# Second score pass of an attention kernel: 64 contraction rows, two chunks on two row tiles

## The chip, the cores and the metric

The kernel runs on one core of a Trainium2 chip. The metric is the device time of one execution in microseconds (us). The engines are named as in the profile: PE is TensorE's matmul side, PEld its weight loads, DVE is VectorE, ACT is ScalarE, POOL is GpSimd, SP is SyncE, which issues nearly all DMAs here.

## The reference, cut to what matters

The program is a two-layer trunk over 1024 latent and 256 context tokens of width 1024. Layer 0 is a recurrent unit beside a spatial gating unit; layer 1 is a gated convolution beside differential attention. Only the attention's scores are touched. There are 4 heads; each has two score maps (m = 0 and 1) with a head dimension of 64, and all 1280 tokens as keys:

```python
def diff_attention(q, k, v, lam):
    s = jnp.einsum('bqhmd,bkhmd->bhmqk', q, k).astype(jnp.float32) * (DIFF_HEAD_DIM ** -0.5)
    p = jax.nn.softmax(s, axis=-1)
    a = p[:, :, 0] - lam * p[:, :, 1]
    return jnp.einsum('bhqk,bkhe->bqhe', a.astype(v.dtype), v)
```

## The kernel before, in words

Every float32 operand of a large matmul is split into two halves that the array takes at its fast float32r rate: a high half (the value rounded, by an ACT copy) and a low half (the value less the high half, by DVE or POOL). A product is then three passes, high by high, high by low and low by high.

The scores use the small head dimension for this. `load_k` (L885 to L892) loads the 64 rows of a head's map twice, into partitions 0 to 63 and again into 64 to 127 of `kd`. An ACT copy rounds all 128 rows into `kt` (L890), and DVE then overwrites rows 64 to 127 with the low half (L891). So `kt` holds the high half of the keys over their low half. `load_q` (L902 to L910) doubles the query rows in the same way, and splits them into `qh` and `ql`, which have the same 64 rows twice. One matmul of `qh` against `kt` over 128 rows therefore sums query-high by key-high and query-high by key-low.

`scores(i, m, st)` (L935 to L952) makes the scores of 128 queries against 1280 keys in one PSUM tile `psc`, of which there is one buffer. The keys go in three chunks, of 256, 512 and 512 columns (`CHUNKS`, L28). For each chunk a matmul with `qh` (L942) is followed by one with `ql` (L943), both over all 128 rows. Then DVE takes the row maximum of all 1280 columns (L944), and ACT the exponentials into `e` (L946). The next call writes `psc` again, so its first matmul waits until ACT has read it.

The loop at L1013 runs over 32 blocks of 128 queries, i, with two calls of `scores` each, and two more rounds for the pipeline's end. That is 64 calls. Between the calls stand the transposes of the combined maps (`trans`, L954), the product with the values (`av`, L968), and `fill(us)` (L916). `fill` takes steps of three matmuls from the other projections of layer 1 (generators of `proj1_g`, L174 to L176) until a fixed budget of time, written in `FL`, is used up. The budgets are constants. What the fillers have left at the end runs behind the attention (L1068). `load_k` of the next head is called behind a head's last two calls of `scores`.

TensorE's instructions run in the order in which they are written (`manual_schedule`, L55). The other engines' order is chosen by the framework's own timeline at build.

Elsewhere in the program, in layer 0, some small matmuls take part of the array's columns: `mod_mm` (L208 to L211) puts four matmuls with 32 weight columns each on four column tiles (`tile_position=(0, r)`), and L462 (`gatep`) has 2 weight columns. They stand between the large matmuls of layer 0's projections, as the steps of a generator do.

Of the kernel before, what the change touches and what calls it, by code (L numbers as in the profile page):

```python
# [11 lines left out]
F32R = mybir.dt.float32r  # L12
AF = mybir.ActivationFunctionType
# [14 lines left out]
CHUNKS = ((0, 256), (256, 512), (768, 512))  # L28
# [14 lines left out]
def tile_hybrid_trunk(es: ExitStack, tc: tile.TileContext, A, out, scr=None):  # L43
    nc = tc.nc
    V, S, G, T, SY = nc.vector, nc.scalar, nc.gpsimd, nc.tensor, nc.sync

    def pool(name, space=None, **kw):
        if space is not None:
            kw["space"] = space
        return tc.tile_pool(name=name, bufs=1, reuse_waits="tile", **kw)  # L50

    def f32(ap):
        return ap.bitcast(F32)
# [189 lines left out]
        split(hi, lo, raw, le=le)  # L243
        return hi, lo

# [1 line left out]
    pj_cm = pool("pj", PSUM)  # L247
    pj = pj_cm.__enter__()

    def pj3(name):  # L250
        t = pj.tile([128, 1536], F32, name=name, tag="pj", bufs=2)
        return t
# [77 lines left out]

    WC = 1282

# [1 line left out]
    lru_cm = ExitStack()  # L334
    lb, ld = lru_cm.enter_context(pool("lrub")), lru_cm.enter_context(pool("lrud"))
    with pool("lrua") as lp, pool("lruc") as lc:
# [167 lines left out]
        p = pj3("pu")  # L504
# [3 lines left out]
        while blocks or late:  # L508
            mod_step()

# [1 line left out]
    vp_cm = pool("sguv", side="right")  # L512
    vp = vp_cm.__enter__()
    so_cm = tc.manual_schedule(engines={nc.sync.engine})
# [5 lines left out]
    p = pj3("pz")  # L520
# [9 lines left out]
    with pool("sguw") as vw:  # L530
# [52 lines left out]
        p = pj3("pu")  # L583
# [72 lines left out]
        G.tensor_tensor(bs[:, 15:16], bs[:, 14:15], cm05[:, 0:1], op=ALU.pow)  # L656
        return bs[:, 12:13], bs[:, 15:16]

# [1 line left out]
    g1 = const.tile([128, KT, 2], F32, name="g1")  # L660
    b1 = const.tile([128, KT, 2], F32, name="b1")
    V.tensor_tensor(g1, mod1[:, :, 1, :], P("lng0")[:, :, None].to_broadcast([128, KT, 2]), op=ALU.mult)
# [66 lines left out]
    woa_cm.__exit__(None, None, None)  # L729
    po_cm.__exit__(None, None, None)  # L730

# [1 line left out]
    mask = [(i + 16) % 32 for i in range(32)]  # L733
    pa_cm, pb_cm = pool("pa", PSUM), pool("pb", PSUM)
    pbp, pa = pb_cm.__enter__(), pa_cm.__enter__()
# [1 line left out]
    def pb(name):  # L737
        t = pbp.tile([128, 512], F32, name=name, tag="pb", bufs=2)
        return t
# [64 lines left out]
    for t in range(NT):  # L804
        p = pb("pv")
# [5 lines left out]
    kv_cm.__exit__(None, None, None)  # L811
    hc_cm.__exit__(None, None, None)

# [1 line left out]
    def proj_qg(hd):  # L815
        w = wload(A["w_in1"][16 + hd])
        qf = rt("qf")
        for c0 in (0, 512):
            p = pb("pq")
            yield from proj1_g(p, w, CTX + c0, 512)  # L820
            x = qf[:, c0:c0 + 512]
            S.activation(x, p, AF.Copy, scale=0.125)
            rope(x, c0, pp)
            SY.dma_start(q_d[hd][:, c0:c0 + 512], x)
        w = wload(A["w_in1"][24 + hd])
        sg = cs.tile([128, LAT], F32, name="sg8", tag="sg8", bufs=1)
        for c0 in (0, 512):
            p = pb("pg8")
            yield from proj1_g(p, w, CTX + c0, 512)
            s = sg[:, c0:c0 + 512]  # L830
            S.activation(s, p, AF.Tanh, scale=0.5)
            V.scalar_tensor_tensor(s, s, 1.0, p, op0=ALU.add, op1=ALU.mult)
            SY.dma_start(g_d[hd][:, c0:c0 + 512], s)
# [37 lines left out]
    ap = ab_cm.__enter__()  # L871
# [13 lines left out]
    def load_k(hd, m):  # L885
        kd = ap.tile([128, NTOK], F32, name="kd", tag="kd", bufs=1)
        for i in range(2):
            SY.dma_start(kd[64 * i:64 * i + 64], k_d[hd][64 * m:64 * m + 64])
        kt = ap.tile([128, NTOK], F32R, name=f"k{m}")
        S.activation(kt, kd, AF.Copy)  # L890
        V.tensor_tensor(kt[64:128], kd[64:128], f32(kt[64:128]), op=ALU.subtract)  # L891
        KS[m] = kt  # L892

    def load_v(hd):
        vf = ap.tile([128, NT, 128], F32, name="vf", tag="kd", bufs=1)
# [28 lines left out]
    KS, VS, QS, AH, OF, SD = {}, {}, {}, {}, {}, {}  # L924
# [10 lines left out]
    def scores(i, m, st):  # L935
        hd, pr, u = i // 8, i % 8 // 2, i % 2
        qh, ql = QS[hd, pr]
        cu = slice(128 * u, 128 * u + 128)
        p = pa.tile([128, 1536], F32, name="psc", tag="psc", bufs=1)
        for c, n in CHUNKS:  # L940
            o = p[:, 256 + c:256 + c + n]
            T.matmul(o, qh[:, m, cu], KS[m][:, c:c + n], start=True, stop=False)  # L942
            T.matmul(o, ql[:, m, cu], KS[m][:, c:c + n], start=False, stop=True)  # L943
        V.tensor_reduce(st[:, m:m + 1], p[:, 256:1536], axis=AX.X, op=ALU.max, negate=True)  # L944
        e_ = ap.tile([128, NTOK], F32, name="e", tag="e", bufs=3)
        S.activation(e_, p[:, 256:1536], AF.Exp, bias=st[:, m:m + 1], scale=1.0, accum_out=st[:, 2 + m:3 + m])  # L946
        if m == 1:
            V.reciprocal(st[:, 5:6], st[:, 3:4])
            V.scalar_tensor_tensor(st[:, 6:7], st[:, 5:6], st[:, 2:3], nlam, op0=ALU.mult, op1=ALU.mult)
            V.scalar_tensor_tensor(SD[i // 4][:, i % 4:i % 4 + 1], st[:, 2:3], EPS, st[:, 2:3], op0=ALU.mult,  # L950
                                   op1=ALU.mult)
        return e_  # L952
# [54 lines left out]
    run(proj_qg(0))  # L1007
    fillers += [proj_qg(1), conv_branch(0), proj_qg(2), conv_branch(1), proj_qg(3), conv_branch(2), conv_branch(3)]
    load_k(0, 0)
    load_k(0, 1)  # L1010
    load_v(0)
    E0, fin = {}, None
    for i in range(34):  # L1013
        hd, pr, u = i // 8, i % 8 // 2, i % 2
        if i < 32:
            if u == 0:
                QS[hd, pr] = load_q(hd, pr)
            st = ap.tile([128, 8], F32, name="st", tag="st", bufs=3)
            if i % 4 == 0:
                SD[i // 4] = ap.tile([128, 4], F32, name="sd", tag="sd", bufs=2)  # L1020
            E0[i] = scores(i, 0, st)
            if i % 8 == 7 and hd < 3:
                load_k(hd + 1, 0)
# [17 lines left out]
        if i < 32:  # L1041
            e1 = scores(i, 1, st)
            V.scalar_tensor_tensor(E0[i], e1, st[:, 6:7], E0[i], op0=ALU.mult, op1=ALU.add)
            if i % 8 == 7 and hd < 3:
                load_k(hd + 1, 1)
# [25 lines left out]
    pa_cm.__exit__(None, None, None)  # L1071
    pb_cm.__exit__(None, None, None)

# [1 line left out]
    with pool("out1") as op, pool("po1", PSUM) as po:  # L1075
        rows = []
        for i, nm in enumerate(("ln_g", "ln_b")):
# [146 lines left out]
```

## Time and profile before

| what | value |
|---|---|
| median of 3 runs | 1170.76 us (1170.17 to 1171.86) |
| span of the profiled execution | 1170.5 us |
| PE busy, of the whole span | 1132.6 us (97%) |
| stretch of the attention | 630 to 1025 us, 395 us |
| PE busy there | 385.5 us |
| DVE, ACT and POOL busy there | 292.9, 196.6 and 84.8 us |

The stretch of the attention goes from shortly before the first call of `scores` to shortly behind the last transposes. A PE row's duration is longer than its distance to the next row, since matmuls are pipelined: what a matmul costs in a stream is the distance from start to start. A weight load stands in a row of PEld. In the page's groups a time of idling before an instruction, with the engine that ended it, stands behind the second bar.

### The profile page before, as it was taken

What the parts mean: (1) busy time and instruction counts of PE and PEld (TensorE: products, weight loads), DVE (VectorE), ACT (ScalarE), POOL (GpSimd) and SP (SyncE); (2) the same over time, 40 slices, a digit from 0 to 9 for tenths busy, and PEclk for the clock granted to TensorE, in tenths of its full rate; (3) what the DMA queues carried; (4) which work ended last, traced back from release to release, by engine and by line L of the source; (5) the groups of instructions that cost most, each with busy time, mean ns of one, the idle gap of its engine ahead of it and who ended that gap; (6) DMA issues with size and microseconds to landing.
All of it is one profiled execution on the core that took longest, in us unless ns stands there. A gap on an engine that the chain in (4) does not pass through costs nothing.

```text
span 1170.5 us, 14967 instructions
## 1 busy us (share of the span) xinstructions
PE 1132.6 (97%) x5842; PEld 922.0 (79%) x5842; DVE 738.9 (63%) x1007; ACT 440.2 (38%) x685; POOL 329.6 (28%) x200
## 2 busy tenths in 40 slices
PE   6999999899999999999999899999999999999997
PEld 3667777678888888888887788788888788888776
DVE  5677986943411475636104668876777877738897
ACT  3453654621121234342113455544544554413110
POOL 1114212620240132258104311221121321221971
PEclk9999999999999999999999999999999999999999
DMA  9654551230332444243215411322221510126622
GB/s 373 239 182 142 180 176 41 73 130 1 120 104 71 144 139 147 96 136 140 77 45 162 113 55 54 95 76 84 77 76 37 146 62 19 46 72 249 218 99 82
DMA packets 71606, 133.93 MB, mean 114 GB/s; under 512 B 6368, under 2 KB 34912, under 8 KB 70640
## 3 DMA queue, kind: packets, MB, share of 16 engines
q1 hardware_dynamic: 71536, 132.97, 34.3%
q8 instruction: 46, 0.75, 0.3%
q14 instruction: 24, 0.20, 0.1%
HBM read 105.67 MB, written 27.28 MB: 114 GB/s over the span
## 4 chain that ended last, share of the span: by engine, by line
PE 83%; DVE 8%; DMA 3%; ACT 3%; issue 2%; POOL 0%; SPq 0%; POOLq 0%; DVEq 0%; ACTq 0%
PE px L164 5%; PE pu L164 5%; PE pg L164 5%; PE p L174 5%; PE p L175 5%; PE p L176 5%; PE pout L648 4%; PE pout L646 4%; PE pout L647 4%; PE pz L164 4%; PE psc L942 3%; PE pv L198 3%; PE pv L199 3%; PE pv L200 3%; PE psc L943 3%; PE atr L965 3%
## 5 line engine op out<-in xcount | busy, mean ns | idle before, releaser
L141 POOL TENSOR_TENSOR wlo<-wraw,whi 128x512 fp32r<-128x512 f32 x92 | 148.1, 1615 | 458.5 <-ACT whi L138 449.8
L648 PE MATMUL pout<-woh,ylo 128*128 128x512 f32 (+1 forms) x296 | 114.5, 387 | 3.1 <-DVE ylo L141 3.1
L946 ACT ACTIVATE e<-psc,st 128x1280 f32<-128x1280 f32 x64 | 85.1, 1329 | 85.6 <-DVE st L944 85.6
L646 PE MATMUL pout<-woh,yhi 128*128 128x512 f32 (+1 forms) x296 | 114.8, 388 | 0.2
L647 PE MATMUL pout<-wol,yhi 128*128 128x512 f32 (+1 forms) x296 | 114.0, 385 | 0.0
L944 DVE TENSOR_REDUCE st<-psc 128x1 f32<-128x1280 f32 x64 | 95.0, 1485 | 27.8 <-PE psc L943 27.7
L138 ACT ACTIVATE whi<-wraw 128x512 fp32r<-128x512 f32 x92 | 57.2, 628 | 134.3 <-PE p L175 27.7
L174 PE MATMUL p<-hhl,whi 128*128 128x512 f32 x256 | 106.8, 417 | 0.0
L176 PE MATMUL p<-hhl,wlo 128*128 128x512 f32 x256 | 100.7, 393 | 0.0
L175 PE MATMUL p<-hll,whi 128*128 128x512 f32 x256 | 100.5, 393 | 0.0
L942 PE MATMUL psc<-k,qh 128*128 128x512 f32 (+1 forms) x192 | 68.0, 369 | 8.4 <-ACT e L946 8.4
L943 PE MATMUL psc<-k,ql 128*128 128x512 f32 (+1 forms) x192 | 69.3, 361 | 0.0
L138 ACT ACTIVATE ah<-atr 128x512 fp32r<-128x512 f32 (+1 forms) x96 | 48.5, 525 | 51.6 <-PE atr L965 50.6
L648 PEld LDWEIGHTS pout<-woh,ylo 128*128 128x128 f32 x296 | 55.6, 188 | 15.3 <-DVE ylo L141 4.0
L646 PEld LDWEIGHTS pout<-woh,yhi 128*128 128x128 f32 x296 | 55.6, 188 | 12.1 <-DVE zt L610 0.5
L647 PEld LDWEIGHTS pout<-wol,yhi 128*128 128x128 f32 x296 | 55.7, 188 | 11.5
L138 ACT ACTIVATE yhi<-yraw 128x512 fp32r<-128x512 f32 x36 | 22.5, 630 | 103.7 <-PE pout L647 57.6
L141 DVE TENSOR_TENSOR al<-atr,ah 128x512 fp32r<-128x512 f32 (+1 forms) x96 | 55.6, 594 | 5.8 <-ACT ah L138 5.6
L176 PEld LDWEIGHTS p<-hhl,wlo 128*128 128x128 f32 x256 | 48.2, 188 | 10.7
L175 PEld LDWEIGHTS p<-hll,whi 128*128 128x128 f32 x256 | 48.6, 190 | 7.3
L141 DVE TENSOR_TENSOR ylo<-yraw,yhi 128x512 fp32r<-128x512 f32 x36 | 43.2, 1208 | 17.5 <-ACT yhi L138 17.5
L174 PEld LDWEIGHTS p<-hhl,whi 128*128 128x128 f32 x256 | 48.4, 189 | 7.2
(292 smaller groups left out, 2822.2 us busy)
## 6 DMA issues: line engine op xcount, KB each, us to landing
wraw<-in_w_in_dram SPq DMA_DIRECT2D x44, 512.0 KB, 3.7
wm<-in_w_mod_dram SPq DMA_DIRECT2D x64, 256.0 KB, 3.4
wraw<-in_w_out_dram SPq DMA_DIRECT2D x16, 512.0 KB, 3.5
wm<-in_w_mod_dram SPq DMA_DIRECT2D x7, 1024.0 KB
xt<-in_xcT_dram SPq DMA_DIRECT2D x8, 640.0 KB, 9.8
xres<-in_xc_dram SPq DMA_DIRECT2D x10, 512.0 KB, 3.7
kd<-k_d SPq DMA_DIRECT2D x16, 320.0 KB, 4.7
wvr<-in_w_v_dram SPq DMA_DIRECT2D x8, 512.0 KB, 4.4
```

Of the source, the lines that this page charges most:

```text
L138: S.activation(hi, src, AF.Copy)
L141: le.tensor_tensor(lo, src, f32(hi), op=ALU.subtract)
L164: T.matmul(o, wt[:, k % 4], hh[hx][:, k], start=st, stop=sp_)
L174: T.matmul(o, hi[:, k % 4], hh[:, k], start=k == 0, stop=False)
L175: T.matmul(o, hi[:, k % 4], hl_[:, k], start=False, stop=False)
L176: T.matmul(o, lo[:, k % 4], hh[:, k], start=False, stop=k == KT - 1)
L646: T.matmul(o, hi[:, i], wh[:, c], start=first and i == 0, stop=False)
L647: T.matmul(o, hi[:, i], wl[:, c], start=False, stop=False)
L648: T.matmul(o, lo[:, i], wh[:, c], start=False, stop=not first and i == 3)
L942: T.matmul(o, qh[:, m, cu], KS[m][:, c:c + n], start=True, stop=False)
L943: T.matmul(o, ql[:, m, cu], KS[m][:, c:c + n], start=False, stop=True)
L944: V.tensor_reduce(st[:, m:m + 1], p[:, 256:1536], axis=AX.X, op=ALU.max, negate=True)
```

## The change

The second pass with `ql` of the two 512-column chunks is made over 64 rows, with the key's high half only. The product of the query's low half with the key's low half is left out there. The two matmuls are put on two row tiles of the array, the first on rows 0 to 63, the second on rows 64 to 127. As the second needs the key's high half in partitions 64 to 127, `load_k` makes one more tile `kx` by one more ACT copy of 512 columns. The 256-column chunk keeps its two matmuls over 128 rows. The six matmuls of a call are put in another order: the three with `qh`, the small one with `ql`, and then the two on row tiles.

```diff
         kt = ap.tile([128, NTOK], F32R, name=f"k{m}")
         S.activation(kt, kd, AF.Copy)
+        kx = ap.tile([128, 512], F32R, name=f"kx{m}")
+        S.activation(kx[64:128], kd[64:128, 768:1280], AF.Copy)
         V.tensor_tensor(kt[64:128], kd[64:128], f32(kt[64:128]), op=ALU.subtract)
-        KS[m] = kt
+        KS[m] = kt, kx
...
         p = pa.tile([128, 1536], F32, name="psc", tag="psc", bufs=1)
-        for c, n in CHUNKS:
-            o = p[:, 256 + c:256 + c + n]
-            T.matmul(o, qh[:, m, cu], KS[m][:, c:c + n], start=True, stop=False)
-            T.matmul(o, ql[:, m, cu], KS[m][:, c:c + n], start=False, stop=True)
+        kt, kx = KS[m]
+        o0, o1, o2 = (p[:, 256 + c:256 + c + n] for c, n in CHUNKS)
+        T.matmul(o1, qh[:, m, cu], kt[:, 256:768], start=True, stop=False)
+        T.matmul(o2, qh[:, m, cu], kt[:, 768:1280], start=True, stop=False)
+        T.matmul(o0, qh[:, m, cu], kt[:, 0:256], start=True, stop=False)
+        T.matmul(o0, ql[:, m, cu], kt[:, 0:256], start=False, stop=True)
+        T.matmul(o1, ql[0:64, m, cu], kt[0:64, 256:768], start=False, stop=True, tile_position=(0, 0))
+        T.matmul(o2, ql[64:128, m, cu], kx[64:128], start=False, stop=True, tile_position=(64, 0))
```

On PE, at one call of `scores` in the middle of the attention (`psc` the scores, `k` the key tile, rows L174 to L176 a filler's step), the order before is:

```order
L176 MATMUL p_6422<-hhl,wlo 128x512
L942 MATMUL psc<-k_5612,qh 128x256
L943 MATMUL psc<-k_5612,ql 128x256
L942 MATMUL psc<-k_5612,qh 128x512
L943 MATMUL psc<-k_5612,ql 128x512
L942 MATMUL psc<-k_5612,qh 128x512
L943 MATMUL psc<-k_5612,ql 128x512
L174 MATMUL p_6422<-hhl,whi 128x512
```

and with the change, at the same place:

```order
L176 MATMUL p_6430<-hhl,wlo 128x512
L944 MATMUL psc<-k_5616,qh 128x512
L945 MATMUL psc<-k_5616,qh 128x512
L946 MATMUL psc<-k_5616,qh 128x256
L947 MATMUL psc<-k_5616,ql 128x256
L948 MATMUL psc<-k_5616,ql 128x512
L949 MATMUL psc<-kx_5618,ql 128x512
L174 MATMUL p_6430<-hhl,whi 128x512
```

The number of matmuls is the same, six; the last two are those on row tiles, and what stands ahead of and behind the call is as it was.

On ACT, around a load of a head's keys (`k` the rounded keys, `kd` the loaded ones, `ah` a transposed map, `e` the exponentials), the order before is:

```order
L138 ACTIVATE whi<-wraw 128x512
L890 ACTIVATE k_5673<-kd 128x1280
L138 ACTIVATE ah<-atr 128x2x128
L138 ACTIVATE whi<-wraw 128x512
L946 ACTIVATE e,st<-psc,st 128x1280
```

and with the change:

```order
L138 ACTIVATE whi<-wraw 128x512
L890 ACTIVATE k_5679<-kd 128x1280
L892 ACTIVATE kx_5681<-kd 64x512
L138 ACTIVATE ah<-atr 128x2x128
L138 ACTIVATE whi<-wraw 128x512
L952 ACTIVATE e,st<-psc,st 128x1280
```

One copy is added directly behind that of `k`, eight times in all. The orders of SP and POOL are the same in both kernels, and DVE's differs in one transposed map's low half, which is one place later.

## Rows read from the trace of the kernel before

**Rows 1.** The page: engines' busy time, the chain's shares by engine, two groups.

```profile
PE 1132.6 (97%) x5842; PEld 922.0 (79%) x5842; DVE 738.9 (63%) x1007; ACT 440.2 (38%) x685; POOL 329.6 (28%) x200
...
PE 83%; DVE 8%; DMA 3%; ACT 3%; issue 2%; POOL 0%; SPq 0%; POOLq 0%; DVEq 0%; ACTq 0%
...
L946 ACT ACTIVATE e<-psc,st 128x1280 f32<-128x1280 f32 x64 | 85.1, 1329 | 85.6 <-DVE st L944 85.6
...
L944 DVE TENSOR_REDUCE st<-psc 128x1 f32<-128x1280 f32 x64 | 95.0, 1485 | 27.8 <-PE psc L943 27.7
```

**Rows 2.** Busy time by stretch, the attention: stretch and length, engines, clock, DMA.

```profile
630.00:1025.00 395.00, 385.50 (x2132) 326.75 (x2131) 292.90 (x409) 196.64 (x327) 84.76 (x55) 0.99 0.26 77
```

**Rows 3.** Who waited for whom, PE in the attention: total us, times, longest.

```profile
PE psc L942 <- ACT e L946: 8.4, 6, 4.8
PE prs L1002 <- POOL rr L994: 1.1, 1, 1.1
```

**Rows 4.** PE in order of time, one call: start, duration, instruction, idle before.

```profile
774.74 0.28 PE L942 MATMUL psc<-k,qh 128*128 128x256 f32 x1
774.86 0.28 PE L943 MATMUL psc<-k,ql 128*128 128x256 f32 x1
774.98 0.40 PE L942 MATMUL psc<-k,qh 128*128 128x512 f32 x1
775.21 0.40 PE L943 MATMUL psc<-k,ql 128*128 128x512 f32 x1
775.45 0.39 PE L942 MATMUL psc<-k,qh 128*128 128x512 f32 x1
775.67 0.40 PE L943 MATMUL psc<-k,ql 128*128 128x512 f32 x1
775.90 0.39 PE L174 MATMUL pq<-hhl,whi 128*128 128x512 f32 x1
```

**Rows 5.** PEld in order of time, the weight loads of the same call.

```profile
775.45 0.19 PEld L943 LDWEIGHTS psc<-k,ql 128*128 128x128 f32 x1
775.68 0.19 PEld L174 LDWEIGHTS pq<-hhl,whi 128*128 128x128 f32 x1
```

**Rows 6.** PE in order of time, a matmul pair with 2 weight columns, layer 0.

```profile
72.33 0.63 PE L164 MATMUL px<-hhl,wlo 128*128 128x512 f32 x2
72.89 1.02 PE L462 MATMUL gatep<-mb,par 128*2 128x512 f32 x2
73.84 0.38 PE L389 MATMUL pgate<-xh,whi 128*128 128x258 f32 x1
74.07 0.29 PE L390 MATMUL pgate<-xo,whi 128*128 128x258 f32 x1
```

**Rows 7.** PEld in order of time, the weight loads of the same place.

```profile
72.89 0.09 PEld L462 LDWEIGHTS gatep<-mb,par 128*2 128x2 f32 x2 [0.37 <-issue]
73.84 0.19 PEld L389 LDWEIGHTS pgate<-xh,whi 128*128 128x128 f32 x1 [0.86 <-ACT whi L138]
73.95 0.19 PEld L390 LDWEIGHTS pgate<-xo,whi 128*128 128x128 f32 x1
```

**Rows 8.** PE in order of time, matmuls on four column tiles between layer 0's.

```profile
102.76 0.63 PE L164 MATMUL px<-hhl,wlo 128*128 128x512 f32 x2
103.32 1.06 PE L211 MATMUL modp<-wm,csil 128*32 128x512 f32 x8
104.32 0.38 PE L164 MATMUL px<-hhc,whi 128*128 128x256 f32 x1
```

**Rows 9.** Groups on PE by shape: count, busy us, mean ns, idle before.

```profile
L942 PE MATMUL psc<-k,qh 128*128 128x256 f32 x64 | 19.8, 310 | 8.4 <-ACT e L946 8.4
L943 PE MATMUL psc<-k,ql 128*128 128x256 f32 x64 | 18.1, 283 | 0.0
```

**Rows 10.** Groups on ACT in the attention, columns as in rows 9.

```profile
L138 ACT ACTIVATE qh<-qd 128x512 fp32r<-128x512 f32 x16 | 10.1, 630 | 10.3 <-PE psc L942 7.7 <-issue 1.4 <-DMA qd<-q_d 1.2
```

**Rows 11.** Busy time by stretch, four short ones, columns as in rows 2.

```profile
642.00:646.60 4.60, 0.00 (x0) 0.00 (x0) 3.85 (x3) 1.31 (x2) 2.97 (x2) 0.99 0.23 63
646.60:650.00 3.40, 3.24 (x9) 2.66 (x10) 1.60 (x6) 0.60 (x3) 1.28 (x1) 0.51 0.85 215
756.50:758.40 1.90, 0.00 (x0) 0.00 (x0) 1.61 (x4) 1.46 (x3) 0.15 (x1) 1.00 0.90 243
...
759.20:766.00 6.80, 6.80 (x21) 5.66 (x20) 5.05 (x8) 2.53 (x4) 2.28 (x2) 0.50 0.23 66
```

## The prediction, made before the changed kernel ran

> **What bounds the kernel now.** I read the page first. PE is busy for 97% of the span and holds 83% of the chain that ended last [rows 1]. So a nanosecond of PE counts, as long as PE has other work to turn to. Next I read the stretch in which the scores lie. In 395 us of attention PE is busy for 385.5; DVE has 292.9, ACT 196.6 [rows 2]. The missing 9.5 us are nearly all explained by two waits: 8.4 us in six waits of a call's first matmul for ACT's exponentials of the call before, the longest 4.8, and 1.1 us once for POOL [rows 3]. The projections fill the time between the calls by a fixed budget, and what is left of them runs behind the attention. So what a call of `scores` takes or gives back on PE goes into the end time nearly one for one.
>
> The third view is one call, in order of time [rows 4]. From its first matmul to the next instruction behind it are 775.90 - 774.74 = 1.16 us. From start to start a 512-column matmul costs 0.23 us (0.92 for four) and a 256-column one 0.12. The durations of 0.40 and 0.28 are longer, since the end of one overlaps the next: a matmul starts some 0.17 us before the record of the one ahead ends (775.67 + 0.40 = 776.07, against 775.90). The weights are loaded ahead: those for the matmul at 775.90 begin at 775.68, while the matmul before runs [rows 5]. No weight load is on the path.
>
> **What the change saves.** Two second passes of 512 columns, 0.46 us, become two that may run side by side on two halves of the array. The nearest row for this is on column tiles: in layer 0 eight matmuls on four column tiles take 1.06 us [rows 8], where two of the same columns on a single tile take 1.02 [rows 6]. Six more matmuls cost 0.04, so some 0.01 for each further one beside the first. By that the pair costs 0.23 + 0.01 = 0.24 us and saves **0.22 us** a call, 14.1 us in 64 calls. The other four matmuls only change places, at no cost: all write PSUM ranges that the same call owns, and the first waits for ACT as before.
>
> **What the change adds on PE.** The array goes from whole to halves and back in each call. The trace of before has no row tile. It has the change to a part of the columns and back, in layer 0, and there it isn't free. The record of the last whole-array matmul ends at 72.33 + 0.63 = 72.96. The load for the 2-column matmul starts at 72.89, 0.07 us before that end [rows 6, 7]. In a stream the next matmul itself would have started 0.17 before. So 0.10 us are lost, and only then do the weights begin to load: PEld idles for 0.37 us with nothing to wait for but "issue" [rows 7]. On the way back it is the same. The pair's record ends at 72.89 + 1.02 = 73.91, the next load starts at 73.84, again 0.07 before. The matmul of 258 columns with these weights then lasts 0.38 us where the next one lasts 0.29 [rows 6]: it stands 0.10 us for its weights, as nothing was loaded ahead. The place with four column tiles reads alike: 102.76 + 0.63 = 103.39 against 103.32, and 0.38 us for the first matmul behind [rows 8]. One change of the array's form thus costs 0.10 + 0.10 = 0.20 us, with 128 columns of weights behind it. A call would have two, **0.40 us**.
>
> The bounds for a row tile's change are 0 (a stream goes on as in rows 5) and 0.20 us. I take 0.20: it is the only change of form that this trace shows, and it reads the same on the way in and out. The Trainium skill, in TensorEngine Tiling (Array Packing), section Tiling Modes (Key Properties), says that changing the tiling mode, not merely the tile, drains TensorE. That would extend the same cost to row tiles; no row here shows it for them. The sum by that page is the one by the upper bound.
>
> **The sum on PE.** A call goes from 1.16 to 1.16 - 0.22 + 0.40 = 1.34 us. In 64 calls +0.18 each are **+11.5 us**.
>
> **What is given back.** The 0.20 us on the way back lie between a call's last matmul and the next call, beside the DVE maximum (1.485 us) and ACT's exponentials (1.329 us, rows 1) on which that next call waits. The six waits shrink by up to 0.20 each, 1.2 us [rows 3]. Besides, a call's first matmul takes 310 ns in the mean where the second takes 283 [rows 9]: 27 ns by 64 are 1.7 us, where a late release kept the weights from being loaded ahead. With more slack I take half of that, 0.8. Together **-2.0 us**, with bounds of 0 and -2.9.
>
> **The extra copy.** `kx` is one ACT copy of 512 columns, eight times. The nearest row, a copy of that width, takes 630 ns [rows 10], so 5.0 us if all of it were on the path, and nothing if all is hidden. Queued behind it on ACT are a transposed map, a weight split or the exponentials of a call. ACT is busy for half of the attention [rows 2], and the next head's keys are loaded ahead of need, so I take **+0.5 us**. The buffer `kd` is held by DVE's longer subtraction anyway, and the DMA issues on SP keep their order. DVE's one instruction in another place has no price.
>
> In all 1170.5 + 11.5 - 2.0 + 0.5 = 1180.5 us for the profiled execution. The median of the runs is 0.3 us over its span, so I forecast **1180.8 us**, 0.9% slower.
>
> **Rivals.** *The change of form is free for row tiles (faster).* Both tiles take the whole width of the array in columns, and the weights could go into it ahead as in rows 5. The call then falls to 0.94 us, the waits stay, and the time is 1170.8 - 14.1 + 0.5 = 1157.2 us. The point at which the sign turns is 0.11 us for one change. For it speaks that every change seen here cuts the columns, not the rows. Against it, the lost time is the same for a 2-column matmul and for 32-column tiles. The page TensorE: Matmul & The Clock Gate of the Trainium skill, Part 2 (the XBUS picture), speaks for it: column tiling takes further operand buses, row tiling none. No run here shows that, and by it the time would be near this rival's.
>
> *Half of it is paid.* If PE loses the 0.10 us but the weights are in place, a call costs 0.20 - 0.22 = -0.02 us, in all -1.3 us, and with the copy the time is 1170.0 us: no change.
>
> *The pair's weights load one after the other.* Two loads of 128 columns start 0.11 us apart (73.84 and 73.95, rows 7). If the second matmul must wait for that, 64 calls cost 7.0 us more: 1187.8 us.
>
> *The row tiles don't run side by side.* Then the change doesn't do what it says; the 0.22 us aren't saved, and the time is 1180.8 + 14.1 = 1194.9 us. Rows 8 speak against it, if column tiles are a guide.
>
> One thing can blur any of these. Behind the two longest waits, 4.6 us and 1.9 us with PE at rest in the stretches read, TensorE's clock was granted at half, 1.2 instead of 2.4 GHz (0.51 and 0.50), for 3.4 and 6.8 us [rows 11]. Half of that, 1.7 and 3.4 us, is what either costs. I see no reason for it to go: the waits are longer than the 0.20 us that they get back.
>
> **Chances.** The forecast with its serial-load variant gets 0.66 (0.54 and 0.12), no overlap 0.07, the half-paid case 0.07 and the free one 0.20. A difference under 0.2%, 2.3 us, can't be told from no change by a measurement of this kernel. Faster: the free case and a little of the half-paid one, 0.23. Same: 0.04. Slower: 0.73. The likeliest's own range is 1176 to 1188 us: up to it by the serial loads (or by less relief and 4.5 us more of copies), down to it by a change of form at 0.16 us instead of 0.20, 128 times. The free case holds 0.20 and I don't want to leave it out beside the tails, so the range goes down to 1157; no overlap, at 1195, is left out.
>
> **What would show it.** If I am right, a call's records show the load of the first row tile 0.07 us before the end of the last whole-array matmul, PEld idle by "issue" ahead of it, the two tile matmuls starting within 0.02 us of each other, and the matmul behind the call lengthened by 0.10; call to next instruction 1.34 us; six waits with less than 8.4 us. A load that begins 0.2 us ahead of its matmul at both edges would prove me wrong, and a call of 0.94 us with it. Tile matmuls 0.23 us apart would be the case without overlap.

## The result, and the profile after

The changed kernel takes 1181.14 us in the median (1178.65 to 1181.88, four runs), the kernel before 1171.31 us beside it. The ratio is 1.0074, with a 95% interval of 1.0061 to 1.0087: 0.7% slower, 8.7 us by the ratio, where 1180.8 us were forecast. A second measurement, told below, gave a ratio of 1.0051 (1.0037 to 1.0065). The profiled execution has a span of 1179.1 us against 1170.5.

The page after, the lines that answer to [rows 1], with line numbers shifted by six (L950 is L944 of before, L952 is L946):

```profile
PE 1141.7 (97%) x5842; PEld 913.0 (77%) x5842; DVE 740.0 (63%) x1007; ACT 445.8 (38%) x693; POOL 326.2 (28%) x200
...
PE 79%; DVE 9%; DMA 5%; ACT 3%; issue 2%; SPq 1%; POOL 0%; POOLq 0%; DVEq 0%; ACTq 0%
...
L952 ACT ACTIVATE e<-psc,st 128x1280 f32<-128x1280 f32 x64 | 85.0, 1328 | 76.6 <-DVE st L950 76.5
L950 DVE TENSOR_REDUCE st<-psc 128x1 f32<-128x1280 f32 x64 | 95.0, 1485 | 29.4 <-PE psc L949 29.1
```

As many matmuls as before, with 128 of them over half of the rows, keep PE busy for 9.1 us more.

One call of `scores` that a filler follows, PE in order of time, columns as in [rows 4]:

```profile
777.58 0.40 PE L944 MATMUL psc<-k,qh 128*128 128x512 f32 x1
777.82 0.40 PE L945 MATMUL psc<-k,qh 128*128 128x512 f32 x1
778.05 0.28 PE L946 MATMUL psc<-k,qh 128*128 128x256 f32 x1
778.17 0.28 PE L947 MATMUL psc<-k,ql 128*128 128x256 f32 x1
778.38 0.49 PE L948 MATMUL psc<-k,ql 64*128 64x512 f32 x1
778.39 0.49 PE L949 MATMUL psc<-kx,ql 64*128 64x512 f32 x1
778.81 0.50 PE L174 MATMUL pq<-hhl,whi 128*128 128x512 f32 x1
779.14 0.40 PE L175 MATMUL pq<-hll,whi 128*128 128x512 f32 x1
```

and the weight loads there, PEld, which answer to [rows 5, 7]:

```profile
778.05 0.19 PEld L947 LDWEIGHTS psc<-k,ql 128*128 128x128 f32 x1
778.38 0.18 PEld L948 LDWEIGHTS psc<-k,ql 64*128 64x128 f32 x1
778.38 0.18 PEld L949 LDWEIGHTS psc<-kx,ql 64*128 64x128 f32 x1
778.81 0.19 PEld L174 LDWEIGHTS pq<-hhl,whi 128*128 128x128 f32 x1 [0.24 <-issue]
778.91 0.19 PEld L175 LDWEIGHTS pq<-hll,whi 128*128 128x128 f32 x1
```

Both edges read as in layer 0. The record of the last whole-array matmul ends at 778.17 + 0.28 = 778.45, and the tiles' loads start at 778.38, 0.07 before. The pair's records last 0.49 where a 512-column matmul lasts 0.40: each stands 0.09 us for its weights. They end at 778.88, the next load starts at 778.81, again 0.07 before, and the filler's first matmul lasts 0.50 instead of 0.40. Inside the pair all is side by side: the two loads and the two matmuls start 0.01 us apart or less.

A call that transposes follow, which is 26 of the 64:

```profile
783.83 0.40 PE L944 MATMUL psc<-k,qh 128*128 128x512 f32 x1
...
785.05 0.66 PE L971 MATMUL atr<-ident,e 128*128 128x128 f32 x4
785.47 0.48 PE L174 MATMUL pq<-hhl,whi 128*128 128x512 f32 x1
```

Here the four transposes' record is 0.66 us long. Behind a call of the kernel before it is 0.60 us:

```profile
769.94 0.39 PE L943 MATMUL psc<-k,ql 128*128 128x512 f32 x1
770.17 0.60 PE L965 MATMUL atr<-ident,e 128*128 128x128 f32 x4
```

So the way back costs 0.06 us for weights there, not 0.10. Both calls are typical. From a call's first matmul to the next instruction behind it the median is 1.23 us over all calls of the changed kernel, where before it is 1.16 to 1.17; the instruction behind then holds PE for 0.34 instead of 0.23 us in the 38 calls with a filler, and for 0.41 instead of 0.35 in the 26 with transposes.

The waits of PE in the attention, as in [rows 3]:

```profile
PE psc L944 <- ACT e L952: 7.4, 5, 4.4
PE prs L1008 <- POOL rr L1000: 0.8, 1, 0.8
```

and the groups that answer to [rows 9], the first matmul of a call and the second, now both of 512 columns:

```profile
L944 PE MATMUL psc<-k,qh 128*128 128x512 f32 x64 | 27.1, 423 | 7.6 <-ACT e L952 7.4
L945 PE MATMUL psc<-k,qh 128*128 128x512 f32 x64 | 25.4, 396 | 0.0
```

The waits for ACT are 1.0 us shorter than in the profile before. The first matmul is still 27 ns longer than the second in the mean.

### The profile page after: what moved, and what is told of

Read it like the earlier page. It is cut to its first block, busy times and chain, and to the rows that moved or that the text cites. A ratio compares the mean times of both kernels' runs of the same rounds, so it can differ in the third digit from the quotient of the medians.

```text
span 1179.1 us, 14974 instructions
## 1 busy us (share of the span) xinstructions
PE 1141.7 (97%) x5842; PEld 913.0 (77%) x5842; DVE 740.0 (63%) x1007; ACT 445.8 (38%) x693; POOL 326.2 (28%) x200
## 4 chain that ended last, share of the span: by engine, by line
PE 79%; DVE 9%; DMA 5%; ACT 3%; issue 2%; SPq 1%; POOL 0%; POOLq 0%; DVEq 0%; ACTq 0%
PE px L164 5%; PE p L174 5%; PE pg L164 5%; PE pu L164 5%; PE p L175 5%; PE p L176 4%; PE pz L164 4%; PE pv L198 3%; PE pv L199 3%; PE pv L200 3%; PE atr L971 3%; PE pout L648 3%; PE pout L647 3%; PE pout L646 3%; PE psc L948 2%
## 5 line engine op out<-in xcount | busy, mean ns | idle before, releaser
L141 POOL TENSOR_TENSOR wlo<-wraw,whi 128x512 fp32r<-128x512 f32 x92 | 145.2, 1583 | 471.5 <-ACT whi L138 446.5
L952 ACT ACTIVATE e<-psc,st 128x1280 f32<-128x1280 f32 x64 | 85.0, 1328 | 76.6 <-DVE st L950 76.5
L950 DVE TENSOR_REDUCE st<-psc 128x1 f32<-128x1280 f32 x64 | 95.0, 1485 | 29.4 <-PE psc L949 29.1
L174 PE MATMUL p<-hhl,whi 128*128 128x512 f32 x256 | 109.4, 427 | 0.0
L176 PE MATMUL p<-hhl,wlo 128*128 128x512 f32 x256 | 100.5, 393 | 0.0
L174 PEld LDWEIGHTS p<-hhl,whi 128*128 128x128 f32 x256 | 48.2, 188 | 12.5 <-issue 6.1
L176 PEld LDWEIGHTS p<-hhl,wlo 128*128 128x128 f32 x256 | 48.0, 188 | 10.7
L198 PE MATMUL pv<-wvh,hhl 128*128 128x512 f32 x128 | 52.0, 406 | 0.0
L971 PE MATMUL atr<-ident,e 128*128 128x128 f32 x320 | 51.9, 276 | 0.0
```

Source lines behind the costliest of these rows:

```text
L141: le.tensor_tensor(lo, src, f32(hi), op=ALU.subtract)
L174: T.matmul(o, hi[:, k % 4], hh[:, k], start=k == 0, stop=False)
L176: T.matmul(o, lo[:, k % 4], hh[:, k], start=False, stop=k == KT - 1)
L198: T.matmul(p, hh[:, k], wh, start=k == 0, stop=False)
L971: T.transpose(p[:, 128 * q:128 * q + 128], e0[:, 128 * (t0 + q):128 * (t0 + q) + 128], ident)
```

## Experiments

Runs of one kernel differ by up to 7 us, in part with the share of time that TensorE's clock was granted at half. Beside the ratio each experiment therefore has an estimate that is meant to take this out: the span times the mean granted clock, averaged over the kernel's runs (for the profiled run of the changed kernel 1179.1 by 0.992, 1169.7 us). It treats the whole span as if it followed the clock, which only PE's part does. For the kernel before it is 1158.2, 1158.5 and 1158.6 us in three sets of 7, 17 and 17 runs. Single runs still scatter in it, from 1165.1 to 1169.7 us in the four of the changed kernel, so a difference of 2 us between two small sets says little.

| kernel | median us | ratio to before (95%) | span by clock, us |
|---|---|---|---|
| changed | 1181.14 | 1.0074 (1.0061 to 1.0087) | 1167.7 |
| changed, again | 1177.45 | 1.0051 (1.0037 to 1.0065) | 1167.2 |
| both on one tile | 1192.66 | 1.0174 (1.0158 to 1.0190) | 1180.6 |
| four changes of form | 1218.12 | 1.0389 (1.0367 to 1.0411) | 1203.0 |
| pair first | 1178.27 | 1.0047 (1.0033 to 1.0061) | 1168.3 |
| whole array, copies unread | 1177.85 | 1.0044 (1.0029 to 1.0060) | 1162.7 |
| whole array, copies read | 1172.38 | 0.9998 (0.9989 to 1.0006) | 1159.0 |
| without the pair | 1146.32 | 0.9792 (0.9760 to 0.9824) | 1137.3 |
| fewer changes in layer 0 | 1169.30 | 0.9983 (0.9970 to 0.9996) | 1155.3 |

**Both on one tile.** The pair is made one behind the other on rows 0 to 63.

```diff
-        T.matmul(o2, ql[64:128, m, cu], kx[64:128], start=False, stop=True, tile_position=(64, 0))
+        T.matmul(o2, ql[0:64, m, cu], kt[0:64, 768:1280], start=False, stop=True, tile_position=(0, 0))
```

> Both 64-row matmuls of the second pass on the same row tile (rows 0 to 63), one behind the other; no second copy of the keys' high half. My theory: the two tiles overlap in the changed kernel and save 0.22 us a call, so here the call is longer by 0.22 us, 64 calls are 14.1 us, and the time is 1181.1 + 14.1 = about 1195 us. Rival A (the overlap is worth little, since what ends late in a call is the change of the array's form): within 3 us of the changed kernel. Rival B (the copies of the keys cost part of the loss): under 1193 us, as they are gone here.

1192.66 us, where about 1195 were expected. By the span and clock it is 13 us over the changed kernel, 0.20 us a call. A call of it on PE:

```profile
703.49 0.50 PE L946 MATMUL psc<-k,ql 64*128 64x512 f32 x1
703.82 0.39 PE L947 MATMUL psc<-k,ql 64*128 64x512 f32 x1
704.15 0.50 PE L174 MATMUL p<-hhl,whi 128*128 128x512 f32 x1
```

From the first tile matmul to the next whole one are 0.66 us, in the changed kernel 778.81 - 778.38 = 0.43. The overlap is worth 0.23 us a call, 14.7 us; PE's waits for ACT are 1.0 us shorter, 6.4 against 7.4. Rival A falls. Rival B named under 1193 us, and by the median alone it isn't refuted; the run with the copies read, below, decides that.

**Four changes of form.** The small matmul over the whole array goes between the two on tiles.

```diff
-        T.matmul(o0, ql[:, m, cu], kt[:, 0:256], start=False, stop=True)
         T.matmul(o1, ql[0:64, m, cu], kt[0:64, 256:768], start=False, stop=True, tile_position=(0, 0))
+        T.matmul(o0, ql[:, m, cu], kt[:, 0:256], start=False, stop=True)
         T.matmul(o2, ql[64:128, m, cu], kx[64:128], start=False, stop=True, tile_position=(64, 0))
```

> The 256-column second pass over the whole array is put between the two matmuls on row tiles, so that a call has four changes of form instead of two, and the two row tiles can't overlap. My theory: each change costs 0.10 us of drain and up to 0.10 us of weights, so two more are +0.36 to +0.40 us and the lost overlap +0.22 us a call: 64 times 0.58 to 0.62 is 37 to 40 us, 1218 to 1221 us. Rival (the cost is paid once for a call that uses tiles, whatever the number of changes): +14 us for the lost overlap alone, 1195 us.

1218.12 us, and 35 to 36 us over the changed kernel by span and clock. The end of a call of it, PE and then PEld:

```profile
703.31 0.28 PE L946 MATMUL psc<-k,qh 128*128 128x256 f32 x1
703.52 0.50 PE L947 MATMUL psc<-k,ql 64*128 64x512 f32 x1
703.95 0.38 PE L948 MATMUL psc<-k,ql 128*128 128x256 f32 x1
704.26 0.49 PE L949 MATMUL psc<-kx,ql 64*128 64x512 f32 x1
704.68 0.66 PE L971 MATMUL atr<-ident,e 128*128 128x128 f32 x4
```

```profile
703.52 0.18 PEld L947 LDWEIGHTS psc<-k,ql 64*128 64x128 f32 x1 [0.24 <-issue]
703.95 0.19 PEld L948 LDWEIGHTS psc<-k,ql 128*128 128x128 f32 x1 [0.25 <-issue]
704.26 0.18 PEld L949 LDWEIGHTS psc<-kx,ql 64*128 64x128 f32 x1
704.68 0.42 PEld L971 LDWEIGHTS atr<-ident,e 128*128 128x128 f32 x4 [0.24 <-issue]
```

Each of the four starts its load late, with "issue" as the reason in three of them. The three matmuls last 0.09 to 0.10 us longer than in a stream, the transposes 0.06. The cost goes with the number of changes, and the rival of a cost paid once falls.

**Pair first.** The two tile matmuls stand at the head of the call, the four others behind them.

```diff
+        T.matmul(o1, ql[0:64, m, cu], kt[0:64, 256:768], start=True, stop=False, tile_position=(0, 0))
+        T.matmul(o2, ql[64:128, m, cu], kx[64:128], start=True, stop=False, tile_position=(64, 0))
...
-        T.matmul(o1, ql[0:64, m, cu], kt[0:64, 256:768], start=False, stop=True, tile_position=(0, 0))
-        T.matmul(o2, ql[64:128, m, cu], kx[64:128], start=False, stop=True, tile_position=(64, 0))
```

> The changed kernel with the two row-tile matmuls at the head of each call, ahead of the four over the whole array. There are still two changes of form per call, one now at its start and one inside. My theory: nearly the same time as the changed kernel, 1178 to 1183 us. The first change falls where PE sometimes waits for ScalarE anyway (five or six waits), which hides 0.1 us each there; the change back stands ahead of a 512-column matmul and its 128 columns of weights in all 64 calls, where behind the call it stood ahead of a transpose in 26 of them (whose weights held it up for 0.06 us instead of 0.11): +1.3 us. Rival (what counts is that the change of form lies behind the last matmul, between it and VectorE's maximum): 1176 us or less.

1178.27 us, inside the range of my theory. By span and clock it is 0.6 to 1.1 us over the changed kernel, near the 1.3 expected but within the scatter. Where in the call the changes of form stand decides little.

**Whole array, copies unread.** The changed kernel's order and copies, with all six matmuls over 128 rows.

```diff
-        T.matmul(o1, ql[0:64, m, cu], kt[0:64, 256:768], start=False, stop=True, tile_position=(0, 0))
-        T.matmul(o2, ql[64:128, m, cu], kx[64:128], start=False, stop=True, tile_position=(64, 0))
+        T.matmul(o1, ql[:, m, cu], kt[:, 256:768], start=False, stop=True)
+        T.matmul(o2, ql[:, m, cu], kt[:, 768:1280], start=False, stop=True)
```

> The changed kernel's order of matmuls and its copies of the keys' high half, but all six matmuls over 128 rows of the whole array; the copies are made and not read. My theory: the loss is all in the two changes of form per call, order and copies cost 0 to 0.5 us, so 1171.3 to 1172 us, no PEld idling by issue at the calls. Rival (copies on ScalarE or the new order delay the chain from maximum to exponentials): 1174 us or more, with longer waits of a call's first matmul than 8.4 us.

1177.85 us: my expectation missed, and at first sight the rival had won, half of the loss without a single row tile. But the experiment had brought in something of its own. ACT in order of time, at the second call:

```profile
648.52 0.59 ACT L822 ACTIVATE qf<-pq 128x512 f32<-128x512 f32 x1
656.89 0.63 ACT L892 ACTIVATE kx<-kd 64x512 fp32r<-64x512 f32 x1 [7.78 <-DMA kd<-k_d]
657.54 1.33 ACT L952 ACTIVATE e<-psc,st 128x1280 f32<-128x1280 f32 x1
```

Nothing reads the copies here, and the third one, for the next head, stands far ahead in ACT's queue. It waited 7.8 us for a load, with the second call's exponentials behind it. PE then waited 3.4 us and ran the third call at half clock (0.50 granted from 658.5 to 664.5):

```profile
659.01 0.79 PE L944 MATMUL psc<-k,qh 128*128 128x512 f32 x1 [3.39 <-ACT e L952]
```

In the changed kernel no such rows stand there.

**Whole array, copies read.** The copy holds half of the rounded keys in all 128 partitions, and the last chunk's second pass takes it, so that it stands in ACT's queue where the change has it.

```diff
-        S.activation(kx[64:128], kd[64:128, 768:1280], AF.Copy)
+        S.activation(kx, kd[:, 768:1280], AF.Copy, scale=0.5)
...
-        T.matmul(o2, ql[:, m, cu], kt[:, 768:1280], start=False, stop=True)
+        T.matmul(o2, ql[:, m, cu], kx, start=False, stop=True)
```

> As the run with the whole array, but the copies of the keys are read, so that they stand in ScalarE's queue where the changed kernel has them: each copy holds half of the rounded keys in all 128 partitions, and the second pass of the last chunk takes it over 128 rows of the whole array (the two halves sum to query-low by key-high). Order of the matmuls as in the changed kernel, no row tile. The run with unread copies had one copy that stood in the queue ahead of the second call's exponentials and waited for a load, 4.8 us late. My theory: that was all of its loss; here 1172 to 1174 us, the exponentials of the second call start 0.1 us behind the maximum. Rival (copies or order cost 4 to 5 us in the changed kernel too): 1176 us or more.

1172.38 us, a ratio of 0.9998, with an interval that spans 1.3 us below the kernel before to 0.7 us above it. Order and copies cost nothing that can be measured; the loss is with the row tiles. PE's waits in the attention:

```profile
PE psc L944 <- ACT e L952: 7.3, 5, 4.4
PE prs L1008 <- POOL rr L1000: 1.1, 1, 1.1
```

**The changed kernel again**, beside that run.

> The changed kernel itself, on the same chip as the run with the copies that are read. By the trace of the changed kernel, 64 calls cost 0.12 to 0.17 us more and the waits give 0.8 us back: 7.5 to 8 us over the same calls without row tiles, so 1180 us, 7 to 9 us over the run with the copies read. By the rival that order and copies make half of the loss: 4 to 5 us over it.

1177.45 us, 5 us over the run with the copies read by the medians, 8.1 by span and clock. My theory's 1180 us missed: by the medians the rival's 4 to 5 us fits better, though its cause, order and copies, costs nothing by the run before this one. Its six runs fall into two groups, four of 1177.0 to 1177.6 us at a mean granted clock of 0.992 or 0.993, and two of 1181.6 and 1182.0 at 0.990. The run with the copies read had 0.988 to 0.993, eleven times. With the clock taken out the two sets of the changed kernel agree (1167.7 and 1167.2), and so do the three of before.

The traces of these two runs give the same without that estimate. From the first row of the scores to the start of the last one are 380.2 us with the copies read and 391.1 us here, 10.9 more. PE worked at half clock for 3.4 us there and some 9.1 us here; half of the difference, 2.9 us, is an estimate of what that costs. There remain 8 us. PE's waits here:

```profile
PE psc L944 <- ACT e L952: 7.0, 4, 4.5
PE prs L1008 <- POOL rr L1000: 0.8, 1, 0.8
```

Whether the change itself also alters how often the clock is halved stays open: its mean granted clock is 0.9912 over ten runs, that of before 0.9896 over 41.

**Without the pair.** The two second passes of 512 columns are left out, the other four matmuls stay.

> The second pass of the two 512-column chunks is left out altogether; four matmuls of a call remain, no row tile and no change of form. The copies of the keys are made and not read. This measures what a microsecond of PE in a call is worth at the end. My theory (PE bounds the stretch, nearly one for one): 0.46 us a call less than the kernel before, 64 times is 29.4 us, 1171.3 - 29.4 = 1142 us, at most 3 us of it given back in waits. Rival (VectorE's and ScalarE's chain from maximum to exponentials bounds the calls): half of it or less, 1157 us or more, with the waits of a call's first matmul far over 8.4 us.

1146.32 us, by the medians 25.9 less than before, of 29.4 that PE no longer works; by the ratio it is 24.4, by span and clock 20.9. So of each microsecond of PE in a call 0.7 to 0.9 reaches the end, and the rival's half or less falls. PE's waits in the attention rise from 9.5 to 13.1 us, a little more than the 3 us expected; so it is PE that bounds the calls, and the chain behind it begins to show. Here too a copy without a reader waited in ACT's queue for its load, 3.8 us, and 1.5 us of PE's waits follow it.

**Fewer changes in layer 0.** The kernel before, with each block's eight modulation matmuls in one go instead of two, and 128 weight columns for the gate's matmul instead of 2 (only the two rows of before are read).

```diff
-            for k in range(4):
+            for k in range(8):
...
-            mod_mm(p, wm, range(4))
-            return p
+            return wm
...
-                T.matmul(pg[0:2, :], sel, mb, start=True, stop=True)
+                T.matmul(pg, selw, mb, start=True, stop=True)
```

> The kernel before, with fewer changes of the array's form in layer 0: the two halves of each block's modulation (four matmuls each on four column tiles) are made in one go of eight, and the gate's matmul takes 128 weight columns instead of 2, with the same two rows of its result read. Scores as before the change. My theory: 12 groups on part of the array fewer, each with two changes of about 0.12 and 0.20 us: 12 times 0.32 is 3.8 us, so 1171.3 - 3.8 = 1167.5 us, unless the eight loads in one go come late, and the gate's matmul shows its weights loaded ahead, with no PEld idling by issue. Rival (changes of form in layer 0 cost nothing at the end, or later loads eat it): 1171 us or more.

1169.30 us, a ratio of 0.9983 (0.9970 to 0.9996): 2.0 us less by the ratio and 3.2 by span and clock, of 3.8 expected. The gate's place, PEld and PE, against [rows 6, 7]:

```profile
71.54 0.31 PEld L164 LDWEIGHTS px<-hhl,wlo 128*128 128x128 f32 x2
71.89 0.42 PEld L456 LDWEIGHTS gatep<-mb,par 128*128 128x128 f32 x2
```

```profile
71.66 0.62 PE L164 MATMUL px<-hhl,wlo 128*128 128x512 f32 x2
72.12 1.02 PE L456 MATMUL gatep<-mb,par 128*128 128x512 f32 x2
72.58 0.68 PE L389 MATMUL pgate<-xh,whi 128*128 128x258 f32 x1
73.10 0.28 PE L390 MATMUL pgate<-xo,whi 128*128 128x258 f32 x1
```

With 128 columns of weights the load starts while the matmul before runs, 0.23 us ahead, and the matmul starts 0.16 us before the record ahead of it ends (72.28), as in a stream. The "issue" ahead of the gate's load in [rows 7] is gone. From the gate's first matmul to the second one behind it are 73.10 - 72.12 = 0.98 us, in [rows 6] 74.07 - 72.89 = 1.18, so the way back is 0.20 us shorter; with 0.10 on the way in that is 0.30 us: what cost time there was the part of the array, not the matmul. The run's time doesn't tell the gate's share from that of the modulation in one go. It is under the kernel before by less than a single run can show.

## Why the prediction was right, step by step

**PE bounds the stretch:** right in the main, by the run without the pair: 0.7 to 0.9 of what PE is spared reaches the end.

**The pair saves 0.22 us:** right. The tiles start within 0.01 us, and undoing the overlap cost 0.23 us a call. The two cases in which they would not, or would load one behind the other, are refuted.

**A change of form costs 0.20 us:** the mechanism was right, the size too large by a little. On the way in it is nearly as forecast: the first tile matmul starts 0.09 us later than in a stream (778.38, where 778.17 + 0.12 is 778.29) and stands 0.09 for its weights. On the way back it holds before a filler: the call takes from 777.58 to 778.81 and 0.10 more, 1.33 us, against 1.16, so +0.17. In 26 calls transposes follow, and they lose 0.06 us on their weights instead of 0.10: 785.05 - 783.83 + 0.06 = 1.28 us, +0.12. Together 38 by 0.17 and 26 by 0.12 are 9.6 us, where the sum had 11.5. The term that was mis-sized is the price of the way back: I took one price for whatever follows the call. One of the rows that it rested on was weaker than I said: the load at 73.84 in [rows 7] is put down to ACT's `whi`, not to "issue". That ACT row had ended at 73.09, 0.75 us before, so the reading stands.

**Given back, -2.0:** mostly wrong. Between the two profiles the waits for ACT shrank by 1.0 us of the 1.2 forecast, from 8.4 to 7.4. But with the copies read, where the calls are no longer than before, they are 7.3 too, so most of that isn't the work of longer calls. Against that run the changed kernel's second profile has 0.3 us less of these waits and 0.3 less of the one for POOL. The 0.8 for weights that would be loaded ahead didn't come: the first matmul's 27 ns are still there.

**The copies, +0.5:** nothing that can be measured, by the run in which they are read; 0.5 us is within its interval.

The records thus give 9.6 us of work on PE less some 0.6 of waits, +9.0 us, where the sum had +10.0. The two sets of the changed kernel give 8.6 to 9.5 us by span and clock, 8.7 and 6.0 by the ratios. That the forecast met the median of 1181.14 so closely is in part luck: the rise was put too high, the level too low. I started from 1170.8 us, where the kernel before took 1171.31 beside the changed one and 1172.2 to 1172.4 in the later sets, and the second set of the changed kernel came to 1177.45. The 0.3 us between span and median were no property of the kernel either: in the runs of before that list both, the time is 1.75 to 2.10 us over the span, so the profiled execution was slower than the three runs whose median I took.

**The rivals on the other side:** the free change of form is refuted by the pair's rows, the half-paid one too: neither edge has its weights loaded ahead. The Trainium skill's rule that I leant on (TensorEngine Tiling (Array Packing), section Tiling Modes, Key Properties: a change of the tiling mode drains TensorE) holds here for row tiles too, with 0.10 us of drain and 0.06 to 0.10 us of weights behind it. The case of the same skill for row tiles, that they take no further operand buses (TensorE: Matmul & The Clock Gate, Part 2), is shown by no run here; whatever the buses do, the drain isn't spared.

**The clock:** I saw no reason for the half-rate stretches to go. In the profile after the clock is at half for 6.8 us around the end of the first long wait (647.7 to 654.5, with PE at work for 5.2 of them), and not behind the second, where before had 6.8. I take this for an accident of one execution, since the wait is still 1.8 us long and the same kernel's second profile has a half-rate stretch there again.

## What to carry to other kernels

Putting small contractions on tiles of the array saves the overlapped streams, and pays twice for each group of them that stands between whole-array matmuls: here 0.10 us of drain and up to 0.10 us of weights at each edge, against 0.22 us saved. By that estimate a group has to hold some two such overlapped pairs before it breaks even, so collect them or leave them on the whole array; no run here had a larger group. A matmul with few weight columns pays at both edges too, and widening its weights to 128 columns took 0.30 us off at the gate's place. An experiment that leaves an instruction without a reader may move that instruction in its queue: keep it read. A gain between two profiles belongs to the change only if a run without the change's own part doesn't show it too, as the shorter waits here did.

## What the runs showed of the hardware beyond that

Two weight loads on the two row tiles start at the same time to 0.01 us and last 0.18 us each, where one load of the whole array lasts 0.19: they don't queue behind each other. Runs of one kernel lie up to 7 us apart, in part with the mean granted clock: in the second set of the changed kernel 1177.0 us at 0.992 to 0.993 against 1182.0 at 0.990, in the first set 1180.93 at 0.992 and 1178.65 at 0.990. What set the number of half-rate stretches in a run stays open. In the attention those of these profiles go with waits of PE of 1.8 to 5.3 us, but behind several waits of 1.8 to 1.9 us there is none.
